# Sums of squares, gate projection and sample products of a two-layer hybrid decoder step: fewer, fuller matmuls, and a redrawn order

## The chip, the cores and the metric

The kernel runs on one core of a Trainium2 chip. The metric is the device time of one execution in microseconds (us); shorter is better. The core has a matrix engine (PE, with its weight loads listed apart as PEld), a vector engine (DVE), a scalar engine (ACT), a general engine (POOL) and a queue that issues the transfers (SP).

## What is computed

One inference step of a trunk with two layers, for 512 prompt tokens and 64 sample tokens (8 sequences of 8), 1024 channels wide, all in float32:

```
for i in 0, 1:
    h = rms_norm(x, norm_mix_pre[i])
    m = pool_mixer(h) if i == 0 else gdn_mixer(h)
    x = x + rms_norm(m, norm_mix_post[i])
    h = rms_norm(x, norm_ffn_pre[i])
    x = x + rms_norm(swiglu(h), norm_ffn_post[i])     # 2816 hidden channels
rms_norm(x, g) = x * rsqrt(mean(x * x) + 1e-6) * g
```

`gdn_mixer` projects h to q, k (8 heads of 128), v, z (16 heads of 128) and two gate columns per v head, runs a gated delta rule (for the prompt in chunks, with the inverse of a triangular matrix; for a sample group as one 64-row system on a given state) and projects back.

## The kernel before

Activations lie with channels on the 128 partitions and the 576 tokens along the free axis, cut into two halves (256 and 320 tokens, `HALVES`, or 288 and 288, `EVEN`). Every large product is three matmuls of rounded parts (`mm3`, line 882): a float32 operand is split into a high and a low part by ACT and DVE (`Weights.split`, line 874; `split2`, line 893), `hH`, `hL` for activations and `wh`, `wl` for weights. One such matmul is one record in the profile; a matmul on unsplit float32 operands is two records, shown as x2.

The program runs in stages: pooling mixer (0 to about 75 us), feed-forward 0 (to 445), GDN mixer with its four head groups G (to 1065), output projection and feed-forward 1 (to 1500), and the tail.

**Norms.** `add_sq` (line 901) squares eight channel blocks on ACT and adds the first seven into `nacc`; the eighth square stays in `nsq`. `rstd` (line 922) reduces both over the partitions with one-column matmuls against `ones`, two (256 tokens) or three (288, 320) places with two matmuls each, takes the root on ACT and the reciprocal on DVE (`nrc`), lays the result on a diagonal (`ndg`, two DVE operations) and spreads it to all partitions with one matmul `ones` x `ndg` into `ps_n`. It is called 12 times; `finish1` (line 2076) does the reduction alone, twice.

**Gates.** `gates` (line 1347) projects h on 32 columns (`wab`): 8 blocks of 3 matmuls into 32 partitions of `ps_g`, for each of the halves, then six small transposes of `abt`.

**Samples.** In `sample_front` (line 1585) the decay products take two matmuls on 64 rows (`gts` with the high and the low part of g), and k and q of the samples (`qks`) are multiplied by k and by `ident` in two column halves of the array each. In `sample_heads` (line 1649) `Ts` x `rs` are products on 64 rows. `Ts` is part of the tile `TQ`.

**The order.** The code only records operations. `Plan.finish` (line 389) then sets each engine's order with a list scheduler that has its own costs, starting from 40 random rounds and then refined once for each string in `CHOSEN` (four strings of window numbers and seeds, `refined`, line 438). Operations named `EITHER` go to DVE or POOL as it decides. Where the plan leaves PE waiting it puts matmuls `ps_w<-ones` that nobody reads (line 432). All recorded instructions are issued from line 436, so the profile is read by tile names.

Of the kernel before, what the change touches and what calls it, by code (L numbers as in the profile page):

```python
# [11 lines left out]
F32 = mybir.dt.float32  # L12
# [44 lines left out]
class Plan:  # L57
# [660 lines left out]
def hybrid_kernel(  # L718
# [69 lines left out]
    sp = pool("gsmp")  # L788

    bet = sp.tile([P, SP1, VH], F32, name="bet")  # L790
    gH = sp.tile([SMP, VH], F32R, name="gH")
    gL = sp.tile([SMP, VH], F32R, name="gL")
    ngs = sp.tile([P, SPANS, VH], F32, name="ngs")
    gce = sp.tile([P, SP1, VH], F32, name="gce")
# [23 lines left out]
    def masks(tmp):  # L818
# [22 lines left out]
        for h in range(2):  # L841
            q = slice(h * SMP, (h + 1) * SMP)
            DVE.tensor_tensor(s_st[q], s_in[q], ident[q, q], op=sub)
# [1285 lines left out]
```

## Time and profile before

| | |
|---|---|
| median of 3 runs | 1537.5 us (1536.16 to 1543.06) |
| profiled execution | 1546.52 us, span of its instructions 1544.5 us |
| PE, PEld busy | 98%, 95% of the span |
| DVE, ACT, POOL busy | 75%, 54%, 8% |
| instructions | 30415, of them 11879 PE records |

A row of the timeline gives the start, the length until the last of the merged instructions ends, engine, line, operation, the tile written, the tiles read, the shape and the count. Matmuls overlap: the time that one takes from its neighbours is read from its start to the start of the next one, not from its length. In the table by windows each engine has its busy time in the stretch and the number of its instructions; PEclk is the granted PE clock.

### The profile page before, as it was taken

To read this page: it belongs to the slowest core of one execution; us is meant where nothing else is said; L and a number is where in the kernel's file an instruction comes from. 1 tells how busy PE (TensorE), PEld (TensorE's weight loads), DVE (VectorE), ACT (ScalarE), POOL (GpSimd) and SP (SyncE) were. 2 spreads that over 40 slices of the span, in tenths; PEclk is the share of its full clock that TensorE was granted. 3 is DMA by queue.
4 is the path that set the end of the run, shared out by engine and by line. 5 is a ranking of instruction groups with operands and counts; after the bars stand their busy time and mean duration, and the time that the engine had idled before them with its cause. 6 is when DMAs were issued, how large, how long until landed. Compare 5 with 4: busy or idle time off the path is not lost.

```text
span 1544.5 us, 30415 instructions
## 1 busy us (share of the span) xinstructions
PE 1519.8 (98%) x11879; PEld 1465.1 (95%) x11879; DVE 1160.7 (75%) x2288; ACT 831.8 (54%) x1811; POOL 122.7 (8%) x265
## 2 busy tenths in 40 slices
PE   8999999999999999999999999999999999999998
PEld 7999999999999899899899889899999999999997
DVE  6794476658688698998899799557895576767854
ACT  7663443435455764854773764546564453534563
POOL 4210000000011010020121020100110000000000
PEclk9799999999999999999999999999999999999998
DMA  7364322333466533334433543657855433223262
GB/s 187 107 192 131 91 87 85 96 96 102 128 178 164 142 106 104 95 107 135 113 113 107 141 125 111 210 154 212 240 177 147 118 93 99 83 81 109 77 185 94
DMA packets 344902, 197.86 MB, mean 128 GB/s; under 512 B 13547, under 2 KB 337740, under 8 KB 344751
## 3 DMA queue, kind: packets, MB, share of 16 engines
q1 hardware_dynamic: 344759, 195.92, 44.4%
q8 instruction: 93, 1.52, 0.4%
q14 instruction: 50, 0.41, 0.1%
HBM read 165.60 MB, written 30.52 MB: 127 GB/s over the span
## 4 chain that ended last, share of the span: by engine, by line
PE 84%; DVE 10%; ACT 2%; DMA 2%; issue 1%; SPq 0%; DVEq 0%; ACTq 0%
PE ps_B L436 29%; PE ps_A L436 26%; PE ps_m L436 15%; PE ps_s L436 5%; PE ps_k L436 4%; PE ps_x L436 2%; PE ps_n L436 2%; DVE ia L436 2%; DVE wl L436 1%; PE ps_e L436 1%; DVE ii L436 1%; DVE ac L436 1%; DVE Uw L436 1%; PE ps_g L436 0%; DVE nacc L436 0%
## 5 line engine op out<-in xcount | busy, mean ns | idle before, releaser
L436 ACT ACTIVATE wh<-wraw 128x1024 fp32r<-128x1024 f32 (+4 forms) x240 | 233.0, 975 | 220.5 <-PE ps_B L436 82.5
L436 DVE TENSOR_TENSOR wl<-wraw,wh 128x1024 fp32r<-128x1024 f32 (+4 forms) x231 | 257.1, 1117 | 80.9 <-ACT wh L436 47.0
L436 PE MATMUL ps_m<-hH,wh 128*128 128x320 f32 (+1 forms) x832 | 246.4, 309 | 0.2 <-ACT u L436 0.2
L436 PE MATMUL ps_m<-hL,wh 128*128 128x320 f32 (+1 forms) x832 | 245.0, 306 | 0.0
L436 PE MATMUL ps_m<-hH,wl 128*128 128x320 f32 (+1 forms) x832 | 242.9, 307 | 0.3 <-DVE wl L436 0.3
L436 PEld LDWEIGHTS ps_m<-hH,wh 128*128 128x128 f32 x832 | 153.8, 188 | 4.3 <-issue 1.3
L436 PEld LDWEIGHTS ps_m<-hH,wl 128*128 128x128 f32 x832 | 152.8, 188 | 3.5 <-issue 1.4
L436 PEld LDWEIGHTS ps_m<-hL,wh 128*128 128x128 f32 x832 | 153.7, 188 | 2.3 <-issue 0.6
L436 PE MATMUL ps_B<-hL,wh 128*128 128x320 f32 (+1 forms) x444 | 128.2, 304 | 0.0
L436 PE MATMUL ps_B<-hH,wl 128*128 128x320 f32 (+1 forms) x444 | 128.0, 305 | 0.0
L436 PE MATMUL ps_B<-hH,wh 128*128 128x320 f32 (+1 forms) x444 | 127.7, 303 | 0.0
L436 PE MATMUL ps_A<-hH,wh 128*128 128x256 f32 (+1 forms) x432 | 119.3, 290 | 0.5 <-DVE nsq L436 0.5
L436 PE MATMUL ps_A<-hL,wh 128*128 128x256 f32 (+1 forms) x432 | 118.6, 290 | 0.0
L436 PE MATMUL ps_A<-hH,wl 128*128 128x256 f32 (+1 forms) x432 | 118.3, 289 | 0.0
L436 PE MATMUL ps_B<-aH,wl 128*128 128x288 f32 x352 | 99.3, 298 | 0.8 <-DVE wl L436 0.8
L436 PE MATMUL ps_B<-aL,wh 128*128 128x288 f32 x352 | 99.4, 296 | 0.0
L436 PE MATMUL ps_B<-aH,wh 128*128 128x288 f32 x352 | 98.5, 297 | 0.0
L436 PE MATMUL ps_A<-aH,wh 128*128 128x288 f32 x352 | 98.0, 296 | 0.0
L436 PE MATMUL ps_A<-aH,wl 128*128 128x288 f32 x352 | 97.9, 296 | 0.0
L436 PE MATMUL ps_A<-aL,wh 128*128 128x288 f32 x352 | 96.8, 295 | 0.0
L436 PEld LDWEIGHTS ps_B<-hH,wl 128*128 128x128 f32 x444 | 81.7, 188 | 0.9 <-DVE wl L436 0.4
L436 DVE SCALAR_TENSOR_TENSOR ac<-u,cwt,ac 128x600 f32<-128x600 f32 x96 | 80.4, 847 | 2.1 <-ACT ac L436 2.0
(462 smaller groups left out, 4076.2 us busy)
## 6 DMA issues: line engine op xcount, KB each, us to landing
wraw<-in_ffn_w_in_dram SPq DMA_DIRECT2D x77, 512.0 KB
wraw<-in_gdn_w_in_dram SPq DMA_DIRECT2D x56, 512.0 KB
graw<-in_ffn_w_in_dram SPq DMA_DIRECT2D x33, 512.0 KB
wraw<-in_ffn_w_out_dram SPq DMA_DIRECT2D x32, 448.0 KB
wraw<-in_gdn_w_out_dram SPq DMA_DIRECT2D x24, 512.0 KB
wraw<-in_ffn_w_out_dram SPq DMA_DIRECT2D x32, 320.0 KB
St<-in_state_gdn_rec_dram SPq DMA_DIRECT2D x32, 256.0 KB
out_dram<-St SPq DMA_DIRECT2D x32, 256.0 KB
```

Source lines behind the costliest of these rows:

```text
L436: calls[e](*a, **k)
```

## The change

1. `add_sq` adds the eighth square into `nacc` too; `rstd` and `finish1` have one matmul for each place. The diagonal `ndg` is gone: the column `nrc`, repeated 128 times, is the stationary operand of one matmul with `ident` for each block of up to 128 tokens.
2. `gates` loads `wab` by its own transfer and leaves it unsplit; four column groups of 32 take two channel blocks each, 16 float32 matmuls for a half. The turn and the sum over the four groups are six matmuls with `four`, four identities of 32 side by side.
3. Samples: high and low part of g lie on 128 rows (`gHL`), so one matmul does both; k of the samples is written twice side by side in `qks`, so each product is one matmul of the whole array; `rs` is written into `vs`, whose upper rows are zeroed at the start of each group, and is multiplied by the whole of `TQ`, whose corner is zeroed once.
4. `CHOSEN` has six strings with other numbers, so the whole order is redrawn.

```diff
@@ -77,112 +77,207 @@
     CHOSEN = (
-        "0: 67429 51633 92322 87354 32076 56101 80323 73026 43122 46420 11460 16617 76499; 1: 86614 42759 48104; "
...
+        "0: 51633 4180 93590 78750 34477 23530 63076 77272 88530 16072 91213 50029 90818 92607 6488 48788 652 "
@@ -829,8 +923,7 @@
         DVE.tensor_copy(s_gt2[:, SMP:], s_gt)
-        s_gt_r = cst.tile([SMP, P], F32R, name="s_gt_r")
-        DVE.tensor_copy(s_gt_r, s_gt2)
+        s_gt_r = cst.tile([P, P], F32R, name="s_gt_r")
@@ -841,6 +934,10 @@
             DVE.tensor_tensor(s_st[q], s_in[q], ident[q, q], op=sub)
+            for c in range(2):
+                DVE.tensor_tensor(s_gt_r[q, c * SMP:(c + 1) * SMP].rearrange("p (b t) -> p b t", b=NB),
+                                  t_gt[q, q].rearrange("p (b t) -> p b t", b=NB),
+                                  seqm2[q].unsqueeze(2).to_broadcast([SMP, NB, NT]), op=mult)
@@ -906,10 +1003,7 @@
             ACT.activation(sq, src, AF.Square)
-            if c == NC - 1:
-                acc.append(sq)
-            else:
-                EITHER.tensor_tensor(acc[0], acc[0], sq, op=add)
+            EITHER.tensor_tensor(acc[0], acc[0], sq, op=add)
@@ -921,28 +1015,25 @@
...
         for i, o in enumerate(offs):
-            for k, a in enumerate(acc):
-                PE.matmul(ps[:, i:i + 1], a[:, o:o + P], ones[:, 0:1], start=k == 0, stop=k == len(acc) - 1)
+            PE.matmul(ps[:, i:i + 1], acc[0][:, o:o + P], ones[:, 0:1], start=True, stop=True)
...
-        dg = halftile(tp, "ndg", hf, 1)
-        DVE.tensor_tensor(dg[:, :256].rearrange("p (i t) -> p i t", i=2), ident.unsqueeze(1).to_broadcast([P, 2, P]),
-                          rc[:, :2].unsqueeze(2).to_broadcast([P, 2, P]), op=mult)
-        if n > 256:
-            DVE.tensor_scalar(dg[:, 256:], ident[:, P - (n - 256):], rc[:, 2:3], None, op0=mult)
-        pr = bank("n%d" % hf.i)[:, :n]
-        PE.matmul(pr, ones, dg, start=True, stop=True)
+        pr = bank("n%d" % hf.i)[:, :hf.n]
+        for i in range(nb):
+            e = min((i + 1) * P, hf.n)
+            PE.matmul(pr[:, i * P:e], rc[:, i:i + 1].to_broadcast([P, P]), ident[:, i * P - offs[i]:e - offs[i]],
+                      start=True, stop=True)
@@ -1359,18 +1450,28 @@
             SP.dma_start(row[:, 1], gdn_dt_bias.to_broadcast([P, VH]))
-            wab = wts.load(w_in, 0, CONV + VDIM, NC, 2 * VH)
-            abt = cp_.tile([2 * VH, T], F32, name="abt", tag="ia", bufs=1)
+            wab = cp_.tile([P, NC, 2 * VH], F32, name="wab", tag="rs", bufs=2)
+            SP.dma_start(wab, w_in[:, CONV + VDIM:].rearrange("(k p) m -> p k m", p=P))
+            abt = cp_.tile([P, T], F32, name="abt", tag="ia", bufs=1)
+            four = cp_.tile([P, 2 * VH], F32, name="four", tag="sn", bufs=1)
+            i4 = ident.rearrange("p (q c) -> p q c", q=4)
+            DVE.tensor_tensor(four, i4[:, 0], i4[:, 1], op=add)
+            for q in (2, 3):
+                DVE.tensor_tensor(four, four, i4[:, q], op=add)
...
                 _, o0, n = hf
-                ps = bank("g")[:2 * VH, :n]
-                mm3(ps, wab, h_of(hf), NC)
+                ps = bank("g")[:, :n]
+                for i in range(4):
+                    for q in range(4):
+                        k = 2 * q + i // 2
+                        PE.matmul(ps[32 * q:32 * q + 32], wab[:, k], h_at(k, o0, n)[i % 2].bitcast(F32),
+                                  start=i == 0, stop=i == 3, tile_position=(0, 32 * q))
...
             for tt in range(SPANS):
-                PE.transpose(ps[:, tt], abt[:, tt * P:(tt + 1) * P], ident[:2 * VH, :2 * VH])
-            PE.transpose(ps[:SMP, SPANS], abt[:, SEQ:], ident[:2 * VH, :2 * VH])
-            PE.matmul(ps[SMP:, SPANS], abt[:, SEQ:], ident[:2 * VH, :2 * VH], start=True, stop=True)
+                PE.matmul(ps[:, tt], abt[:, tt * P:(tt + 1) * P], four, start=True, stop=True)
+            for q in range(2):
+                PE.matmul(ps[q * SMP:(q + 1) * SMP, SPANS], abt[:, SEQ:], four, start=True, stop=True)
@@ -1386,8 +1487,8 @@
                                      op0=mult, op1=mult)
-            DVE.tensor_copy(gH, g[:SMP, SPANS])
-            DVE.tensor_tensor(gL, g[:SMP, SPANS], gH.bitcast(F32), op=sub)
+            DVE.tensor_copy(gHL, g[:, SPANS])
+            DVE.tensor_tensor(gHL[SMP:], g[SMP:, SPANS], gHL[SMP:].bitcast(F32), op=sub)
@@ -1425,8 +1526,9 @@
             vt = gp.tile([P, SPANS, 4, P], F32, name="vt", tag="vt", bufs=2)
-            qks = gp.tile([P, 2, 2, SMP], F32, name="qks", tag="qks", bufs=2)
+            qks = gp.tile([P, 2, 3, SMP], F32, name="qks", tag="qks", bufs=2)
             vs = gp.tile([P, 4, P], F32, name="vs", tag="vs", bufs=2)
+            POOL.memset(vs[SMP:], 0.0)
@@ -1529,11 +1631,15 @@
                     qi = 0 if kind == "k" else 1
-                    dst, dss = qk[:, i, qi], qks[:, i, qi]
+                    dst, dss = qk[:, i, qi], qks[:, i, 2 * qi]
...
                 ACT.activation(dst, ac[:, :SEQ], AF.Silu)
-                ACT.activation(dss.rearrange("p (b t) -> p b t", b=NB), acs, AF.Silu)
+                if kind == "k":
+                    ACT.activation(qks[:, i, :2].rearrange("p x (b t) -> p x b t", b=NB),
+                                   acs.unsqueeze(1).to_broadcast([P, 2, NB, NT]), AF.Silu)
+                else:
+                    ACT.activation(dss.rearrange("p (b t) -> p b t", b=NB), acs, AF.Silu)
@@ -1581,17 +1687,17 @@
         E2 = [slice(0, SMP), slice(SMP, P)]
+        TQ = cp_.tile([P, 2, 2, P], F32, name="TQ")
+        POOL.memset(TQ[SMP:, :, :, SMP:], 0.0)
...
             ps = bank("s")[:, :4 * SMP].rearrange("p (h i) -> p h i", h=4)
-            gts = cp_.tile([SMP, 2, 4, SMP], F32R, name="gts", tag="T01", bufs=1)
-            for i, src in enumerate((gH, gL)):
-                gt = gts[:, i]
-                EITHER.tensor_tensor(gt, s_le.unsqueeze(1).to_broadcast([SMP, 4, SMP]),
-                                   src[:, h4].bitcast(F32).unsqueeze(2).to_broadcast([SMP, 4, SMP]), op=mult)
-                PE.matmul(ps, s_gt_r, gt, start=i == 0, stop=i == 1)
+            gts = cp_.tile([P, 4, SMP], F32R, name="gts", tag="T01", bufs=1)
+            EITHER.tensor_tensor(gts, s_in.unsqueeze(1).to_broadcast([P, 4, SMP]),
+                                 gHL[:, h4].bitcast(F32).unsqueeze(2).to_broadcast([P, 4, SMP]), op=mult)
+            PE.matmul(ps, s_gt_r, gts, start=True, stop=True)
@@ -1601,9 +1707,9 @@
                 pt = pk[:, P:2 * P]
-                for e, q in enumerate(E2):
-                    PE.matmul(pkv[q], qks[:, hd, 0], qks[:, hd], start=True, stop=True, tile_position=(0, e * SMP))
-                    PE.matmul(pt[q], qks[:, hd, 0], ident, start=True, stop=True, tile_position=(0, e * SMP))
+                kk = qks[:, hd, :2].rearrange("p x t -> p (x t)")
+                PE.matmul(pkv, kk, qks[:, hd, 1:], start=True, stop=True)
+                PE.matmul(pt, kk, ident, start=True, stop=True)
@@ -1674,7 +1780,8 @@
                 sn = cp_.tile([P, 4, 2, P], F32, name="sn", tag="sn", bufs=1)
-                rs, t1, vn = sn[lo, 0], sn[up, 1], sn[:, 2]
+                rss = vs[:, 2 * hd:2 * hd + 2]
+                rs, t1, vn = rss[lo], sn[up, 1], sn[:, 2]
@@ -1685,7 +1792,7 @@
                 for e in range(2):
-                    PE.matmul(pv[:, 0, e * P:(e + 1) * P], Ts[:, hd, e], rs[:, e], start=True, stop=True)
+                    PE.matmul(pv[:, 0, e * P:(e + 1) * P], TQ[:, hd, e], rss[:, e], start=True, stop=True)
@@ -2081,9 +2187,9 @@
                 n = n if i == 2 else P
-                for k, a in enumerate(acc):
-                    PE.matmul(ps[:n, i:i + 1], a[:, i * P:i * P + n] if i < 2 else a[:, EV - n:], ones[:, 0:1],
-                              start=k == 0, stop=k == len(acc) - 1)
+                a = acc[0]
+                PE.matmul(ps[:n, i:i + 1], a[:, i * P:i * P + n] if i < 2 else a[:, EV - n:], ones[:, 0:1],
+                          start=True, stop=True)
```

The array's work in the order, by kind: `ps_n<-ones,nsq` 38 matmuls before and none now; `ps_n<-ndg,ones` 12 and none; `ps_n<-ident,nrc` none and 32 (24 of 128 columns, 8 of 32 or 64); `ps_w<-ones` 31 and 42. ACT's table loads are 25 and 30.

PE at the first norm of the program (`ps_n_240`, `ps_n_244`: its reduction and its spread; `ps_B` belongs to the pooling of the second half), before:

```order
L436 MATMUL ps_n_240<-ones,nacc 128x1
L436 MATMUL ps_n_240<-ones,nsq 128x1
L436 MATMUL ps_B<-bm_146,xn 128x128
L436 MATMUL ps_B<-bh_148,xn 128x15
L436 MATMUL ps_B<-dH,wh 128x320
L436 MATMUL ps_B<-bm_146,xn 128x128 x2
L436 MATMUL ps_B<-bh_148,xn 128x15 x2
L436 MATMUL ps_B<-bm_146,xn 128x128
L436 MATMUL ps_B<-bh_148,xn 128x15
L436 MATMUL ps_B<-dL,wh 128x320
L436 MATMUL ps_B<-dH,wl 128x320
L436 MATMUL ps_n_244<-ndg,ones 128x256
```

The same norm now (`ps_n_239`, `ps_n_242`):

```order
L531 MATMUL ps_n_239<-ones,nacc 128x1
L531 MATMUL ps_B<-bm_145,xn 128x128
L531 MATMUL ps_n_239<-ones,nacc 128x1
L531 MATMUL ps_B<-dH,wh 128x320
L531 MATMUL ps_B<-bh_147,xn 128x15
L531 MATMUL ps_B<-bm_145,xn 128x128
L531 MATMUL ps_B<-dL,wh 128x320
L531 MATMUL ps_B<-dH,wl 128x320
L531 MATMUL ps_B<-bh_147,xn 128x15
L531 MATMUL ps_n_242<-ident,nrc 128x128 x2
```

The reductions over `nsq` are gone, and two matmuls with `nrc` stand in place of the one with `ndg`. PE in the gates, before (a stretch out of 24 such rows for the first half):

```order
L436 MATMUL ps_g<-hH,wl 32x256
L436 MATMUL ps_g<-hH,wh 32x256
L436 MATMUL ps_g<-hL,wh 32x256
L436 MATMUL ps_g<-hH,wl 32x256
L436 MATMUL ps_g<-hH,wh 32x256
```

and now, the whole of the first half:

```order
L531 MATMUL ps_m<-hH,wl 128x320
L531 MATMUL ps_g<-hH,wab 32x256 x4
L531 MATMUL ps_g<-hL,wab 32x256 x4
L531 MATMUL ps_g<-hH,wab 32x256 x4
L531 MATMUL ps_g<-hL,wab 32x256 x4
L531 MATMUL ps_x<-ident,qk 128x128 x4
```

Sixteen matmuls in runs of four stand for 24 single ones. PE at the samples' k and q of the first group, before:

```order
L436 MATMUL ps_m<-hL,wh 128x256
L436 MATMUL ps_k<-qks 64x128
L436 MATMUL ps_k<-ident,qks 64x128
L436 MATMUL ps_k<-qks 64x128
L436 MATMUL ps_k<-ident,qks 64x128
L436 MATMUL ps_k<-qks 64x128
L436 MATMUL ps_k<-ident,qks 64x128
L436 MATMUL ps_k<-qks 64x128
L436 MATMUL ps_k<-ident,qks 64x128
L436 MATMUL ps_m<-hH,wh 128x320
```

and now (the second pair of heads stands 53 rows further down):

```order
L531 MATMUL ps_k<-qk 128x256
L531 MATMUL ps_k<-qks 128x128
L531 MATMUL ps_k<-ident,qks 128x128
L531 MATMUL ps_m<-hH,wh 128x320
L531 MATMUL ps_m<-hL,wh 128x320
```

Two matmuls on all 128 columns take the place of four in column halves for each pair of heads.

More of the change, by code (lines that the diff above doesn't have):

```diff
@@ L790, in hybrid_kernel @@
     bet = sp.tile([P, SP1, VH], F32, name="bet")
-    gH = sp.tile([SMP, VH], F32R, name="gH")
-    gL = sp.tile([SMP, VH], F32R, name="gL")
+    gHL = sp.tile([P, VH], F32R, name="gHL")
     ngs = sp.tile([P, SPANS, VH], F32, name="ngs")
@@ L922, in rstd @@
     def rstd(tp, acc, hf, on_dve=False):
-        n = hf.n
-        offs = [0, P] if n == 256 else [0, P, n - P]
+        offs = [0, P] if hf.n == 256 else [0, P, hf.n - P]
+        nb = len(offs)
         ps = bank("n%d" % hf.i)
         for i, o in enumerate(offs):
-            for k, a in enumerate(acc):
-                PE.matmul(ps[:, i:i + 1], a[:, o:o + P], ones[:, 0:1], start=k == 0, stop=k == len(acc) - 1)
-        rc = halftile(tp, "nrc", hf, 1, (P, 4))[:, :len(offs)]
+            PE.matmul(ps[:, i:i + 1], acc[0][:, o:o + P], ones[:, 0:1], start=True, stop=True)
+        rc = halftile(tp, "nrc", hf, 1, (P, 4))[:, :nb]
         if on_dve:
-            v, t = (halftile(tp, w, hf, 1, (P, 4))[:, :len(offs)] for w in ("nv", "nt"))
-            DVE.tensor_scalar(v, ps[:, :len(offs)], 1.0 / D, EPS, op0=mult, op1=add)
+            v, t = (halftile(tp, w, hf, 1, (P, 4))[:, :nb] for w in ("nv", "nt"))
+            DVE.tensor_scalar(v, ps[:, :nb], 1.0 / D, EPS, op0=mult, op1=add)
             rsqrt(rc, v, t)
         else:
-            ACT.activation(rc, ps[:, :len(offs)], AF.Sqrt, bias=eps_c, scale=1.0 / D)
+            ACT.activation(rc, ps[:, :nb], AF.Sqrt, bias=eps_c, scale=1.0 / D)
             DVE.reciprocal(rc, rc)
-        dg = halftile(tp, "ndg", hf, 1)
-        DVE.tensor_tensor(dg[:, :256].rearrange("p (i t) -> p i t", i=2), ident.unsqueeze(1).to_broadcast([P, 2, P]),
-                          rc[:, :2].unsqueeze(2).to_broadcast([P, 2, P]), op=mult)
-        if n > 256:
-            DVE.tensor_scalar(dg[:, 256:], ident[:, P - (n - 256):], rc[:, 2:3], None, op0=mult)
-        pr = bank("n%d" % hf.i)[:, :n]
-        PE.matmul(pr, ones, dg, start=True, stop=True)
+        pr = bank("n%d" % hf.i)[:, :hf.n]
[3 more added lines that the diff above has]
+                      start=True, stop=True)
         return pr
@@ L1661, in sample_heads @@
                     EITHER.tensor_copy(kx.rearrange("p (b w) -> p b w", b=NB)[:, :, x_ * SMP:x_ * SMP + NT],
-                                    qks[:, hd, x_].rearrange("p (b t) -> p b t", b=NB))
+                                    qks[:, hd, 2 * x_].rearrange("p (b t) -> p b t", b=NB))
                 km = cp_.tile([P, NB, P], F32R, name="km", tag="T01", bufs=1)
@@ L1801, in core @@
             out.append(oss)
-            TQ = cp_.tile([P, 2, 2, P], F32, name="TQ", tag="TQ", bufs=1)
             Ts, Qs = TQ[:SMP], TQ[SMP:, :, :, :SMP]
```

305 rows, old and new, of the table CHOSEN are left out of this document.

## The prediction

> **What bounds the kernel now.** I read the page first: busy shares and the chain that ended last.
>
> ```profile
> span 1544.5 us, 30415 instructions
> PE 1519.8 (98%) x11879; PEld 1465.1 (95%) x11879; DVE 1160.7 (75%) x2288; ACT 831.8 (54%) x1811; POOL 122.7 (8%) x265
> ...
> PE 84%; DVE 10%; ACT 2%; DMA 2%; issue 1%; SPq 0%; DVEq 0%; ACTq 0%
> ```
>
> PE carries the end. So an edit counts by the PE time that it takes or gives, as long as nothing else ends last. Whether something does differs by stage. The table by windows, feed-forward 0, GDN mixer, feed-forward 1:
>
> ```profile
> 75.00:445.00 370.00, 369.40 (x2769) 367.55 (x2767) 254.03 (x399) 170.15 (x263) 5.27 (x6) 1.00 0.40 116
> 445.00:1065.00 620.00, 612.23 (x5163) 568.91 (x5163) 525.17 (x1209) 380.73 (x1055) 79.44 (x164) 1.00 0.47 133
> 1065.00:1500.00 435.00, 433.93 (x3274) 431.61 (x3274) 307.60 (x509) 212.35 (x340) 11.64 (x10) 1.00 0.45 132
> ```
>
> In the feed-forward stages the weight loader is busy 99% of the time (367.55 of 370.00, 431.61 of 435.00): PE time removed there is time saved. In the GDN stage PE is listed busy for 612 of 620 us, but the loader for 568.91, 92%; at the feed-forward's share it would be 616. Some 47 us of that stage are PE standing in pipelines, changing shape or waiting, and DVE has 525 us of work there. [...]
>
> A last reading concerns the clock, at the program's start:
>
> ```profile
> 18.00:45.00 27.00, 26.53 (x202) 24.22 (x201) 20.43 (x45) 22.49 (x61) 6.10 (x6) 1.00 0.48 111
> 45.00:62.50 17.50, 17.35 (x69) 15.93 (x69) 10.78 (x29) 9.05 (x25) 2.48 (x3) 0.51 0.32 96
> ```
>
> For 17.5 us the granted clock is half although PE is busy 99%. At full speed that work takes 17.5 x 0.51 = 8.9 us, so the stretch costs 8.6 us.
>
> The profiled execution took 1546.5 us, the median of the runs is 1537.5, 9.0 less. I make the sum against the profile and take it off the median unchanged, since a difference of kernels moves both.
>
> **The norms.** The last reduction of feed-forward 0's first half, three places with two matmuls each (rows between are left out), and its spread:
>
> ```profile
> 440.70 0.28 PE L436 MATMUL ps_n<-ones,nacc 128*128 128x1 f32 x2
> ...
> 441.73 0.36 PE L436 MATMUL ps_n<-ones,nsq 128*128 128x1 f32 x2
> 441.96 0.38 PE L436 MATMUL ps_B<-aL,wh 128*128 128x288 f32 x1
> ...
> 444.99 0.72 PE L436 MATMUL ps_n<-ndg,ones 128*128 128x288 f32 x2
> 445.34 0.51 PE L436 MATMUL ps_B<-aH,wl 128*128 128x288 f32 x1
> 445.69 0.42 PE L436 MATMUL ps_B<-aH,wh 128*128 128x288 f32 x2
> ```
>
> Six reductions take 441.96 - 440.70 = 1.26 us, 0.21 each. The groups show how many there are:
>
> ```profile
> L436 PE MATMUL ps_n<-ones,nsq 128*128 128x1 f32 (+2 forms) x76 | 13.6, 248 | 2.3 <-ACT nsq L436 2.3
> L436 DVE TENSOR_TENSOR ndg<-ident,nrc x12: 418/424/426, 35.6 to 1143.7; 128x256 f32<-128x256 f32 x12
> L436 DVE TENSOR_TENSOR nacc<-nacc,nsq x81: 406/453/2402, 20.7 to 1531.8; 128x288 f32<-128x288 f32 x36, 128x320 f32<-128x320 f32 x23, 128x256 f32<-128x256 f32 x22
> ```
>
> 76 records are 38 matmuls: 38 x 0.21 = 8.0 us removed. The spread before: 445.69 - 444.99 less one ordinary matmul of 0.13 is 0.57, for 12 norms 6.8. For the new spread, a float32 matmul of 128 columns, and below for four column groups, I use this place in the GDN stage:
>
> ```profile
> 620.62 1.93 PE L436 MATMUL ps_k<-St,kx 128*32 128x256 f32 x32
> 622.49 1.13 PE L436 MATMUL ps_k<-S,qk 128*128 128x256 f32 x4
> 623.45 0.61 PE L436 MATMUL ps_s<-vn,QD 128*128 128x128 f32 x4
> 623.90 0.49 PE L436 MATMUL ps_x<-ident,qk 128*128 128x128 f32 x3
> ```
>
> Two of 128 columns take 0.45, 0.225 each; two of 256 take 0.96, 0.48 each. The new spread is 24 x 0.225 + 8 x 0.21 = 7.1, so +0.3. No row loads a column repeated 128 times as weights: below, nothing is gained over an ordinary load, since the moving columns set these 0.225; above, I bound it by doubling, 32 x 0.21 = +6.7. [...] Norms: -7.7 on PE.
>
> On each norm's path one DVE addition of 0.453 comes ahead of the reduction and one `ndg` of 0.424 goes behind it, and half of the reductions go. That is even or a little shorter; beside it PE has other matmuls (441.96 onward), and without that cover it would be 14 x (0.45 - 0.42 - 0.5), a gain, so nothing is counted. DVE, which these queue on, gets 14 and loses 12 such operations.
>
> **The gates.** 48 matmuls in three groups of 16, one group, the step from one to the next, and the turn:
>
> ```profile
> L436 PE MATMUL ps_g<-hH,wl 128*32 128x256 f32 (+1 forms) x16 | 4.7, 294 | 0.0
> ...
> 490.22 0.28 PE L436 MATMUL ps_g<-hH,wh 128*32 128x256 f32 x1
> 490.34 0.28 PE L436 MATMUL ps_g<-hL,wh 128*32 128x256 f32 x1
> ...
> 510.28 0.69 PE L436 MATMUL ps_g<-ident,abt 32*128 32x32 f32 x7
> 510.90 0.42 PE L436 MATMUL ps_m<-hL,wh 128*128 128x320 f32 x1
> ```
>
> 24 of 256 columns at 0.12 and 24 of 320 at 0.14 (from 541.15 to 541.29, below) are 6.2 us. The new form is that of `St,kx`, 16 float32 matmuls of 256 columns in four column groups: 622.49 - 620.62 = 1.87 with the way out. For 320 columns 1.25 times that, 2.34, and twice 0.1 to get in (below): 4.4. The turn, 0.62 before, becomes six whole matmuls at 0.21, 1.3. Gates: 4.4 - 6.2 + 0.7 = -1.1. If the groups did not run side by side, 16 x 0.48 and 16 x 0.60 would be 17.3 us in place of 4.4. The split of `wab` on ACT and DVE goes, three additions for `four` come; neither is on PE's path. The SP queue has as many transfers as before.
>
> **The samples.** Three places of the first group: `gts`, with a run of idle matmuls behind it; `qks`; `TQ`.
>
> ```profile
> 541.15 0.31 PE L436 MATMUL ps_m<-hL,wh 128*128 128x320 f32 x1
> 541.29 0.30 PE L436 MATMUL ps_m<-hH,wl 128*128 128x320 f32 x1
> 541.53 0.50 PE L436 MATMUL ps_s<-gts,s_gt_r 64*128 64x256 f32 x2
> 541.96 0.43 PE L436 MATMUL ps_g<-misc,t_gt 128*128 128x64 f32 x2
> ...
> 542.64 0.94 PE L432 MATMUL ps_w<-ones 128*128 128x128 f32 x6
> 543.35 0.41 PE L436 MATMUL ps_m<-hH,wh 128*128 128x320 f32 x1
> ...
> 566.59 0.28 PE L436 MATMUL ps_m<-hL,wh 128*128 128x256 f32 x1
> 566.80 0.45 PE L436 MATMUL ps_k<-qks 128*64 128x128 f32 x4
> ...
> 567.87 0.41 PE L436 MATMUL ps_m<-hH,wh 128*128 128x320 f32 x1
> ...
> 624.14 0.36 PE L436 MATMUL ps_m<-hH,wh 128*128 128x256 f32 x1
> 624.44 0.71 PE L436 MATMUL ps_s<-sn,TQ 64*128 64x128 f32 x4
> 625.08 0.33 PE L436 MATMUL ps_x<-ident,qk 128*128 128x128 f32 x1
> ```
>
> From the last ordinary matmul to `gts` it is 0.24 where 0.14 is usual: 0.10 to change shape. `gts`: 0.10 + 0.43 becomes one matmul of 0.12, -0.4, four times -1.6. `qks`: 0.09 + 1.07 becomes four matmuls at 0.225, -0.27, four times -1.1. `TQ`: 0.30 - 0.12 + 0.64 becomes two at 0.225, -0.37, eight times -3.0. Samples: -5.7. POOL zeroes half of `vs` once a group, 512 columns as here:
>
> ```profile
> L436 POOL MEMSET eyo<- 128x512 f32 x1 | 0.5, 527 | 9.2 <-PE ps_n L436 9.2
> ```
>
> POOL has 79 us of work in the 620 of this stage and the rows are not needed until the products, so the memset is free; without that cover it is 4 x 0.53 = 2.1. Behind it on POOL queue the copies of the next projection.
>
> **The order.** 42 idle matmuls against 31: three take 543.35 - 542.64 = 0.71, so 11 more are 2.6 us in which the plan itself leaves PE waiting; 12 of them stand in the GDN stage, where the samples and gates are. I count +2.6. What else the redrawn order does no row of before shows: it may take back part of the 47 us, or add to them. I take zero between these. Five more table loads on ACT fall on an engine with 54% of work.
>
> **Sum.** -7.7 - 1.1 - 5.7 + 2.6 = -11.9: 1534.6 for an execution like the profiled one, and 1525.6 for the median.
>
> **The rivals.**
>
> A. The order takes stalls back in the GDN stage as well. For it: 47 us of loader slack there, in a stage in which the order decides what waits. Against: DVE has 85% of that stage in work. A fifth, 9.4 us, gives 1516; a third 1510.
>
> B. The GDN stage doesn't end by PE, and what gates and samples free becomes waiting for DVE. For it: the 12 more idle matmuls there. Only norms and idle matmuls stay: -5.1, 1532.4. This is within 0.5% of before (7.7 us, about what a measurement of this kernel can tell from no change).
>
> C. Slower: the new order leaves stretches so thin in PE work that the clock halves, as at 45 us, but in stages where PE is full. Each stretch like that one costs 8.6 us. Against the gain of 11.9 it decides from the second on; three are +25.8 - 11.9 = +13.9, 1551. For it: PE was busy 98% in the 27 us ahead of that stretch, so listed work doesn't protect. Against: from 75 to 1500 us the three windows show a clock of 1.00 throughout. [...]
>
> D. The change doesn't do what it says: the column groups run one behind the other. 17.3 - 4.4 = 12.9 more, 1538.5. Against: `St,kx` at 620.62.
>
> **How the numbers follow.** My forecast 0.47, A 0.27, B 0.17, C 0.06, D 0.03. The likeliest is the sum: 1525.6. Its own range, with the prices 30% off either way and part of the doubled weight load, is 1521 to 1531. The range adds A down to a loader gain of 15 us, 1511, and B with 3 us of order lost, 1536; C, D and the far end of A stay out, about 0.14. Faster than 1529.8: most of the forecast (0.44), all of A and a little of B, 0.72. Within 0.5%: the rest of the forecast, most of B, and D, 0.22. Slower: C, 0.06.
>
> **What would show it.** In the profile of the changed kernel: no `nsq` row on `ps_n`, `ident,nrc` x64 with about 0.225 from start to start for one matmul; `hH,wab` and `hL,wab` in two runs of about 1.9 and 2.3 us; single `gts`, pairs of `qks`; feed-forward 0 shorter by its norms' reductions only, about 1 us; the GDN stage shorter by some 7 us less the idle matmuls. A GDN stage shorter by over 12 us says A; one as long as before says B; a clock under 1.00 between 75 and 1500 us says C. The prediction is wrong if the feed-forward stages change by more than 5 us, or if the spread takes more than 0.3 a matmul.

## The result, and the profile after

| | before | after |
|---|---|---|
| median | 1537.73 us (4 runs, 1536.16 to 1543.06) | 1525.66 us (4 runs, 1525.06 to 1526.06) |
| profiled execution | 1546.52 us, span 1544.5 | 1525.06 us, span 1523.3 |
| granted clock of that execution | 0.986 | 0.997 |

The ratio is 0.9909 (0.988 to 0.9938 at 95%), so the kernel after is faster, and its median lies 0.06 us from the forecast of 1525.6. That the sum met the median so closely is partly luck, as the rest shows: the work gave about 3 us less than the sum, and the clock, which the sum counted at nothing, gave about 3 us.

The head of the page after, and its chain:

```profile
span 1523.3 us, 30379 instructions
PE 1501.0 (99%) x11850; PEld 1452.8 (95%) x11850; DVE 1155.7 (76%) x2284; ACT 840.6 (55%) x1815; POOL 129.4 (8%) x269
...
PE 88%; DVE 6%; ACT 3%; DMA 2%; issue 1%; POOL 0%; SPq 0%; DVEq 0%; ACTq 0%; POOLq 0%
```

PE still carries the end, 88% of the chain where it was 84%. The same three stretches of the table by windows:

```profile
75.00:445.00 370.00, 369.18 (x2759) 367.98 (x2759) 256.06 (x402) 172.90 (x266) 7.28 (x9) 1.00 0.39 113
445.00:1065.00 620.00, 613.95 (x5223) 574.59 (x5221) 520.86 (x1204) 387.24 (x1058) 84.10 (x162) 1.00 0.48 137
1065.00:1500.00 435.00, 432.94 (x3249) 430.00 (x3249) 306.61 (x502) 215.17 (x345) 11.98 (x13) 1.00 0.44 130
```

In the GDN stretch the loader has 574.59 us where it had 568.91, but the stretches are cut by time, and the one of after holds 16 us more of the output projection. Between the marks below the loader is busy for 544.61 of 594.28 us before and 546.00 of 591.10 after, so its slack there shrank by 4.6 us. The lengths of the stages are read from marks in the timeline: the first feed-forward product, the last `aH` product of feed-forward 0, the last `ps_m`, and the last group of matmuls. Before, then after:

```profile
60.53 0.41 PE L436 MATMUL ps_A<-hH,wh 128*128 128x256 f32 x1
...
467.45 0.30 PE L436 MATMUL ps_B<-aH,wl 128*128 128x288 f32 x1
...
1061.73 0.31 PE L436 MATMUL ps_m<-hH,wl 128*128 128x320 f32 x1
...
1536.64 1.38 PE L436 MATMUL ps_A<-ident,nh 128*128 128x128 f32 x6 [0.20 <-ACT nh L436]
```

```profile
50.74 0.39 PE L531 MATMUL ps_A<-hH,wh 128*128 128x256 f32 x1
...
454.65 0.30 PE L531 MATMUL ps_B<-aH,wl 128*128 128x288 f32 x1
...
1045.75 0.31 PE L531 MATMUL ps_m<-hH,wl 128*128 128x320 f32 x1
...
1515.46 0.95 PE L531 MATMUL ps_A<-ident,nh 128*64 128x128 f32 x6 [0.33 <-ACT nh L531]
```

How much of the difference is due to the clock can be read in the windows of before around its halved stretches, each shown with the 3.4 us ahead of it (the third column from the end is the granted clock):

```profile
41.90:45.30 3.40, 2.86 (x19) 2.21 (x17) 3.40 (x11) 2.97 (x9) 0.00 (x0) 1.00 0.00 0
45.30:62.40 17.10, 17.10 (x67) 15.74 (x68) 10.38 (x29) 8.65 (x23) 2.48 (x3) 0.50 0.32 97
468.60:472.00 3.40, 3.10 (x26) 2.88 (x26) 3.40 (x8) 2.38 (x6) 0.00 (x0) 1.00 0.46 133
472.00:475.40 3.40, 3.40 (x19) 3.40 (x18) 2.43 (x6) 0.38 (x1) 0.00 (x0) 0.50 0.78 202
1499.40:1502.80 3.40, 1.60 (x14) 1.38 (x12) 1.00 (x3) 1.37 (x3) 0.00 (x0) 1.00 0.88 230
1502.80:1509.60 6.80, 6.32 (x32) 6.16 (x33) 5.00 (x9) 2.96 (x7) 0.00 (x0) 0.50 0.31 90
```

After has nothing of the kind from 18 us to its last products:

```profile
18.00:1515.00 1497.00, 1487.27 (x11778) 1440.50 (x11776) 1140.46 (x2237) 827.94 (x1790) 115.86 (x196) 1.00 0.45 128
```

A stretch of 3.4 us would not show in the 1.00 of so long a window (the windows of the forecast hid the one at 472.0 in the same way); in windows of 10 us all those of after from 20 to 1510 us are at 1.00. Both kernels have one more at 11 us, 6.8 long, which cancels. A stretch at half clock costs half its length, if PE has work throughout: at 60.0 us of before a product of 320 columns starts 0.27 us ahead of the next, and 0.14 at full clock. So, in us:

| stage | before | after | difference | of it clock | rest |
|---|---|---|---|---|---|
| to the first feed-forward product | 60.5 | 50.7 | -9.8 | -7.6 | -2.2 |
| feed-forward 0 | 406.9 | 403.9 | -3.0 | -0.9 | -2.1 |
| GDN | 594.3 | 591.1 | -3.2 | -1.7 | -1.5 |
| output projection to the end | 474.9 | 469.7 | -5.2 | -3.4 | -1.8 |
| sum | | | -21.2 | -13.6 | -7.6 |

Of 21.2 us between the two profiled executions 13.6 are halved stretches that only before has. The median of before holds fewer of them. Its 75 runs beside the experiments, grouped by the granted clock that each run lists:

| granted clock | runs of before | median us |
|---|---|---|
| up to 0.9895 | 22 | 1544.9 |
| 0.990 to 0.9925 | 27 | 1539.4 |
| 0.993 to 0.9945 | 17 | 1535.4 |
| 0.995 and above | 9 | 1534.7 |

All ten runs of after (four above, six below) lie between 0.995 and 0.998, with a median of 1525.7. At about equal clock the change is worth 9.0 us, and 3 to 4 us more in the median come from the clock. The runs of after list up to 0.998 and those of before at most 0.996, so these 9.0 still hold a little clock; the traces leave 7.6.

The parts look as the change says. The groups of the norms' matmuls and one spread for 288 tokens, in the timeline:

```profile
L531 PE MATMUL ps_n<-ones,nacc 128*128 128x1 f32 (+2 forms) x76 | 9.7, 229 | 0.0
L531 PE MATMUL ps_n<-ident,nrc 128*128 128x128 f32 (+2 forms) x64 | 9.2, 271 | 0.0
```

```profile
433.79 0.86 PE L531 MATMUL ps_n<-ident,nrc 128*128 128x128 f32 x6
434.48 0.38 PE L531 MATMUL ps_B<-aH,wl 128*128 128x288 f32 x1
```

No row over `nsq` is left, and three spread matmuls take 0.69 us. The gates' two bursts, one `gts` and one pair `vs` x `TQ`:

```profile
502.99 0.64 PE L531 MATMUL ps_g<-hH,wab 128*32 128x256 f32 x8
...
504.86 0.55 PE L531 MATMUL ps_x<-ident,qk 128*128 128x128 f32 x3
...
508.46 0.75 PE L531 MATMUL ps_g<-hH,wab 128*32 128x320 f32 x8
...
510.76 0.44 PE L531 MATMUL ps_x<-ident,qk 128*128 128x128 f32 x2
...
527.48 0.34 PE L531 MATMUL ps_s<-gts,s_gt_r 128*128 128x256 f32 x1
...
612.14 0.75 PE L531 MATMUL ps_s<-vs,TQ 128*128 128x128 f32 x4
612.64 0.39 PE L531 MATMUL ps_m<-hH,wl 128*128 128x320 f32 x1
```

The bursts take 1.87 and 2.30 us (forecast 1.87 and 2.34); two products of `vs` with `TQ` take 0.50 (forecast 0.45).

### The profile page after: what moved, and what is told of

It reads as the page before. It is cut to its first block, busy times and chain, and to the rows that moved or that the text cites. A ratio compares the mean times of both kernels' runs of the same rounds, so it can differ in the third digit from the quotient of the medians.

```text
span 1523.3 us, 30379 instructions
## 1 busy us (share of the span) xinstructions
PE 1501.0 (99%) x11850; PEld 1452.8 (95%) x11850; DVE 1155.7 (76%) x2284; ACT 840.6 (55%) x1815; POOL 129.4 (8%) x269
## 4 chain that ended last, share of the span: by engine, by line
PE 88%; DVE 6%; ACT 3%; DMA 2%; issue 1%; POOL 0%; SPq 0%; DVEq 0%; ACTq 0%; POOLq 0%
PE ps_B L531 29%; PE ps_A L531 26%; PE ps_m L531 19%; PE ps_s L531 5%; PE ps_k L531 5%; PE ps_x L531 2%; PE ps_e L531 1%; DVE wl L531 1%; PE ps_n L531 1%; DVE Uw L531 1%; DMA vt<-z_d 1%; DVE ac L531 1%; ACT wh L531 1%; DMA wraw<-in_gdn_w_in_dram 0%; DMA yo<-y_d 0%
## 5 line engine op out<-in xcount | busy, mean ns | idle before, releaser
L531 PE MATMUL ps_m<-hH,wh 128*128 128x320 f32 (+1 forms) x832 | 251.5, 313 | 0.0
L531 PE MATMUL ps_m<-hH,wl 128*128 128x256 f32 (+1 forms) x832 | 245.8, 308 | 0.1
L531 PEld LDWEIGHTS ps_B<-hH,wh 128*128 128x128 f32 x444 | 81.7, 188 | 0.7 <-ACT wh L531 0.6
```

The lines of the kernel that those rows point to most:

```text
L531: calls[e](*a, **k)
```

## The experiments

**The theory after the result:** the edits free PE time at about the forecast prices; part of it is lost in waits; a second part of the gain is the clock, which from 18 us to the last products halves three times in before, each time behind 3.41 us in which PE moves few columns (1602 to 3084 by its rows, where the median is 7200), and not once in after. **Rivals:** the clock has nothing to do with it; the new order alone made the gain. Twelve kernels ran. Medians stand beside runs of before on the same chip: 1538.82 for e1 to e4, 1538.28 for e5 to e8, 1539.64 for e9 to e12.

### The kernel after once more

> The kernel after once more, unchanged, beside the variants on the same chip. Theory of the clock (half of the gain is PE work, the other half fewer stretches at half clock, which begin at different places from run to run): median 1525 to 1527 against 1538 to 1539 for before, granted clock 0.996 to 0.998 in nearly every run against 0.986 to 0.996 for before. Theory of PE work alone: the same medians, but the kernel before in its runs of the highest clock (0.995) is still 12 us above after. By the clock theory it is 6 to 9 us above after in such runs.

Measured: 1525.50 us (1524.24 to 1528.78), ratio to before 0.992 (0.989 to 0.9949); granted clock 0.995 or 0.996 in its six runs. Before's six runs beside it with 0.995 or more have a median of 1534.5. So the gain at about equal clock is 9, not 12: at the upper end of what the clock theory said. The clock has a part, and the work, edits and order together, has the larger one.

### Prices: one kind of matmul issued twice

Three kernels keep after's order and issue one kind of matmul twice.

```
 calls[e](*a, **k)
+if e == "PE" and self.twice(a):
+    calls[e](*a, **k)
...
+    return out == "ps_n" and l == "nacc"                                     # e1
+    return out == "ps_n" and l == "nrc"                                      # e2
+    return (out, l) in (("ps_k", "qks"), ("ps_s", "s_gt_r")) or (l, r) == ("TQ", "vs")   # e3
```

> The kernel after, in its own order, with each of the 38 one-column matmuls of the norms' reductions issued twice (the same value written twice): as many as the change removed, and at the places where the kept ones stand. Theory 1, PE is full and a matmul costs its own time: 38 x 0.21 = 8.0 us more than the kernel after (1525.7), 1533.7. Rival, the norms' matmuls stand where PE waits for a norm anyway, and the gain came from the order: under 2 us, 1526 to 1527.5. Rival, a norm's path carries them twice over (the matmul and the wait behind it): over 12 us, above 1537.

Measured: 1535.74 us (1531.55 to 1542.25), ratio to before 0.9988 (0.9968 to 1.0008). That is 10.2 over after, but its clock is lower too, 0.990 to 0.996. Its four runs at 0.995 and above have a median of 1534.2, which is 8.7 over after. The trace parts the two: its profiled execution is 15.0 us longer than that of after and holds four halved stretches of 3.4 us that after does not have (from 34.2, 51.3, 727.1 and 1498.5 us). They cost 6.8, and the rest is 8.2, close to the forecast price of 8.0. Two windows of it, and some rows of PE in the first:

```profile
30.80:34.20 3.40, 3.40 (x25) 2.96 (x24) 1.80 (x6) 1.56 (x6) 0.00 (x0) 1.00 0.33 91
34.20:37.60 3.40, 3.40 (x19) 3.40 (x17) 0.93 (x3) 1.32 (x4) 0.12 (x1) 0.50 0.02 5
```

```profile
32.78 0.29 PE L531 MATMUL ps_n<-ones,nacc 128*128 128x1 f32 x2
32.93 0.36 PE L533 MATMUL ps_n<-ones,nacc 128*128 128x1 f32 x2
33.16 0.47 PE L531 MATMUL ps_B<-bm,xn 128*128 128x128 f32 x2
33.46 0.28 PE L531 MATMUL ps_n<-ones,nacc 128*128 128x1 f32 x2
33.60 0.36 PE L533 MATMUL ps_n<-ones,nacc 128*128 128x1 f32 x2
```

PE is listed busy for 3.40 of 3.40 us and the clock halves all the same. What the window holds is work that moves little: reductions of one column each, and products of 64 columns ahead of them, 2278 columns in all by its rows, where the median of such windows in after is 7200. After, without the doubled rows, has a clock of 1.00 there. So the 38 one-column reductions cost 8.2 us of their own, 0.22 each, and beside them this trace lost 6.8 us to the clock.

> The kernel after, in its own order, with each of the 32 matmuls that spread a norm's root by a repeated column issued twice. Theory 1 with an ordinary weight load: 24 x 0.225 + 8 x 0.14 (a narrow one stands between starts 0.14 us apart in the trace of after), 6.5 us more, 1532.2. If a repeated column loads at double price: 13 us more or over, above 1538. If the spread hides in a wait for the norm: under 2 us, below 1527.7.

Measured: 1533.48 us (1530.99 to 1538.04), ratio 0.9972 (0.9955 to 0.9989), median clock 0.996: 8.0 over after, 0.25 for each of the 32 and 1.5 more than the forecast. In the trace one halved stretch more (from 725.7 us) costs 1.7 of the 8.3 us by which its profiled execution is longer; the 6.6 left are 0.21 for each and the forecast of 6.5. So a repeated column loads at about the ordinary price; double price is out.

> The kernel after, in its own order, with the samples' products on whole rows issued twice: 4 of gts, 16 of qks and 16 of vs with TQ, where a product that adds to a bank adds twice (so the samples' part of the output counts double). Theory 1, the GDN stage ends by PE: 4 x 0.12 + 32 x 0.225 = 7.7 us more, 1533.4, all of it between the first gate matmul and the last of ps_m. Rival B, the stage waits for DVE and what PE is given hides: under 2.5 us, 1526 to 1528.

Measured: 1532.52 us (1531.18 to 1535.12), ratio 0.9958 (0.9941 to 0.9974), median clock 0.996: 7.0 over after, forecast 7.7. None of these products adds to what its bank holds, so nothing counts twice in the output. The marks of its GDN stage:

```profile
454.82 0.29 PE L531 MATMUL ps_B<-aH,wl 128*128 128x288 f32 x1
...
1053.63 0.31 PE L531 MATMUL ps_m<-hH,wl 128*128 128x320 f32 x1
```

598.8 us where after has 591.1: 7.7 more, the whole of the forecast, with no halved stretch in the stage of either. What is added to PE in this stage counts in full.

### The idle matmuls, taken away and added

```
 if e is None:
-    self.tc.nc.tensor.matmul(self.banks[i[0]][i[1]][0][:, :self.idle.shape[1]], self.idle, self.idle,
-                             start=True, stop=True)
     continue
```

> The kernel after, in its own order, without its 42 idle matmuls, which write a bank that nothing reads. Theory 1, they stand where the plan leaves PE waiting: between no change (1525.7) and 42 x 0.235 = 9.9 us less (1515.8); by the prediction's count, a quarter of their time on the path, some 2.5 us less, 1523. Rival, they hold the clock: without them the granted clock falls below 1.00 in the GDN stage, 8.6 us for a stretch like the one at 45 us of the kernel before, so 1534 or more.

Measured: 1534.33 us (1531.58 to 1541.15), ratio 0.9966 (0.9947 to 0.9986): 8.8 slower than after with 42 matmuls less, and no run with a clock over 0.994. Two of the four halved stretches in its trace before the end, with the windows ahead of them:

```profile
462.90:466.30 3.40, 2.52 (x21) 2.20 (x19) 3.40 (x7) 1.54 (x4) 0.00 (x0) 1.00 0.29 80
466.30:469.70 3.40, 3.40 (x17) 3.40 (x17) 3.40 (x7) 1.08 (x3) 2.61 (x3) 0.50 0.94 254
531.20:534.60 3.40, 1.94 (x11) 1.32 (x10) 3.40 (x10) 3.36 (x6) 0.92 (x2) 1.00 0.66 191
534.60:538.00 3.40, 3.40 (x17) 3.40 (x17) 2.84 (x14) 2.77 (x7) 1.20 (x3) 0.50 0.85 233
```

The four last 20.4 us together and cost 10.2. The start is no different from that of after, although the page lists no halved stretch there: time ahead of the first record of the clock counts as full. The rows show half speed until 15.8 us, 0.21 us from start to start and then 0.12:

```profile
14.96 0.41 PE L529 MATMUL ps_A<-dL,wh 128*128 128x256 f32 x1
15.17 0.41 PE L529 MATMUL ps_A<-dH,wl 128*128 128x256 f32 x1
...
18.76 0.28 PE L529 MATMUL ps_A<-dL,wh 128*128 128x256 f32 x1
18.88 0.28 PE L529 MATMUL ps_A<-dH,wl 128*128 128x256 f32 x1
```

So the clock accounts for the whole of the 9.6 us between the two profiled executions, and the 42 matmuls themselves cost 10.2 less 9.6, some 0.6 us. The idle matmuls hold the clock, as the rival has it: 0.984 to 0.994 in the twelve runs without them, 0.995 to 0.998 in those of after. What they cost, the 0.6 us, is small beside the 10.2.

The other way round: before, with idle matmuls added where its trace shows thin stretches.

```
 if e in (None, "PE"):
+    for _ in range(self.MORE.get(at, 0) if e else 0):
+        self.more(still, quiet)
+    at += 1
...
+MORE = {186: 2, 188: 1, 400: 2, 3385: 2, 3393: 1, 5921: 6, 10590: 8}
```

> The kernel before in its own order, with 22 more idle matmuls at five places where its trace shows PE waiting and moving few columns (43.3, 82.6, 469.2, 855.2 and 1503.3 us). Nothing else changes. Theory of the clock: thin stretches, in which PE moves few columns within about 3.4 us, halve the clock for the next stretch, and filled ones don't: the granted clock rises to 0.995 or more and the median falls by 4 to 8 us from before's, to 1531 to 1534. Theory of PE work: 22 more matmuls cost between nothing (they stand in waits) and 22 x 0.22 = 4.8 us, the clock stays at 0.992 or so: 1538 to 1543.

Measured: 1536.31 us (1534.24 to 1538.39), ratio 0.9981 (0.9962 to 1.0001). The clock is 0.993 to 0.997 in its twelve runs, and the spread shrinks from 15.3 us in before to 4.2. Three of the five places lie where before's trace was halved; the same three here:

```profile
40.00:62.40 22.40, 22.25 (x170) 20.83 (x169) 21.23 (x60) 16.73 (x41) 3.81 (x5) 1.00 0.48 141
466.00:475.40 9.40, 9.40 (x80) 9.14 (x79) 8.46 (x20) 5.64 (x9) 3.46 (x6) 1.00 0.59 158
1495.00:1510.00 15.00, 15.00 (x122) 14.95 (x121) 9.43 (x16) 6.10 (x11) 0.00 (x0) 1.00 0.56 182
```

All at full clock. So the filled stretches kept the clock in this trace, as the clock theory has it, while the size of the effect was taken too large: the median fell by 2.0, which its interval does not tell from nothing, and not by 4 to 8, since before's median loses some 4 us to the clock, against its runs at 0.995 and above, and the added matmuls cost 1 to 2.

### PE work taken from before, in its own order

```
+if out == "ps_n" and l == "nsq":                                          # e7
+    continue
...
+    thin += 1                                                             # e8, at ps_m<-hH,wl
+    if thin % 16 == 8 and not k["stop"] and not k["start"]:
+        continue
```

> The kernel before in its own order, without the 38 one-column matmuls on the eighth squares (the norms then lack one eighth of their sum). PE work: 38 x 0.21 = 8.0 us less than before, some 1530.5. If these matmuls, which keep PE listed busy and move one column each, also made stretches thin: 2 to 4 us more than that, 1527 to 1529, with the granted clock up to 0.994 or more. If the norms wait for the last square anyway: under 3 us, 1536 or more.

Measured: 1536.88 us (1528.73 to 1541.43), ratio 0.9983 (0.9959 to 1.0006): 1.4 less in the median, and 8.0 less (0.9948) lies outside the interval. Its five runs at 0.995 and above have a median of 1531.0, 3.5 below before's beside them at such clocks, but they spread from 1528.7 to 1538.0. So about half of the 8.0 came through, as far as five runs tell. The clock did not get better: its trace still halves at 45.2 and 468.4 us.

> The kernel before in its own order, without 38 of the 832 correction products of the GDN stage's projection, spread evenly over the stage (21 of 320 columns, 17 of 256). If that stage ends by PE, it gets shorter by 21 x 0.14 + 17 x 0.12 = 5.0 us and the whole falls to 1533.5; what the change gave less than its sum in this stage was then lost by the new order. Rival B, the stage waits for DVE: under 1.5 us less, 1537 or more, and the change could not have had its sum there in any order.

Measured: 1533.38 us (1531.07 to 1540.37), ratio 0.9972 (0.9948 to 0.9995): 4.9 less, as expected if that stage ends by PE. But its four runs at 0.995 and above are at 1532.2, 2.3 below before's, and in its trace the GDN stage is no shorter. Its marks, and the longest entry of PE's waits in that stage, here and in before:

```profile
466.12 0.30 PE L443 MATMUL ps_B<-aH,wl 128*128 128x288 f32 x1
...
1060.04 0.31 PE L443 MATMUL ps_m<-hH,wl 128*128 128x320 f32 x1
```

```profile
PE ps_x L443 <- DVE vt L443: 3.5, 5, 1.2
```

```profile
PE ps_x L436 <- DVE vt L436: 1.6, 1, 1.6
```

593.9 us against 594.3, of which 1.7 were clock. PE waits 3.5 us for `vt` where it waited 1.6. One trace and four runs don't settle the share, between none and all of the 5.0; at equal clock it is about half, and what can be seen of the rest is waits, for DVE above all. Rival B has its part in that.

### Without the refinement

Four kernels with `CHOSEN = ()`: before, after, and before with one edit alone.

> The kernel before with CHOSEN empty: its operations in the order of the 40 random rounds alone, without the refinement by windows. It is the base of the next three. Slower than before by what the refinement gave, which no run shows yet: 1540 to 1600.

Measured: 1563.07 us (1560.66 to 1565.68), ratio to before 1.0153 (1.012 to 1.0186). The refinement of before's order gave 23.4 us.

> The kernel after with CHOSEN empty: the edits of the change in an order that nobody refined. Theory 1, the edits free PE and an order drawn for them turns that into time: 7 to 12 us below the unrefined kernel before. Theory 2, the refinement of the new order made the gain, and the edits alone give nothing: within 3 us of the unrefined kernel before, or slower; two unrefined orders may differ by some us on their own, so between 3 and 7 us stays undecided.

Measured: 1583.26 us (1578.84 to 1585.66), ratio to before 1.0283 (1.0253 to 1.0314): 20.2 slower than the unrefined kernel before. The refinement of after's order gave 58 us. Theory 1 fails in this form: the edits alone, in the order that 40 random rounds happen to find, lose.

> The unrefined kernel before with the norms' edit alone (one reduction a place, the repeated column). In before's fixed order the removal of the reductions gave some 3 us at equal clock, and PE waited for the rest. Theory 1, a newly drawn order uses the rest too: 6 to 8 us below the unrefined kernel before. Rival, the norm's path ends the wait in any order: under 3 us.

Measured: 1565.30 us (1563.26 to 1567.79), ratio to before 1.0168 (1.0136 to 1.02): 2.2 slower than its base, whose runs go from 1560.66 to 1565.68. The ranges overlap, so no difference is shown, and the gain of 6 to 8 us of theory 1 is not there.

> The unrefined kernel before with the samples' edit alone (gts on 128 rows, qks written twice, rs in the zeroed vs times the whole TQ). By the price of the products 5.7 us less; by what the GDN stage kept of a removal in before's order, 0 to 3 us less; theory 2, order alone: anywhere within 5 us of the unrefined kernel before, either way.

Measured: 1581.07 us (1579.93 to 1582.40), ratio to before 1.027 (1.0238 to 1.0302): 18.0 slower than its base, outside of what any theory said. About 5 of the 18 are clock, since its trace holds halved stretches of 17.1 us in all behind the start and that of its base 6.8. No price of a product explains the rest. The four times fall in two pairs: 1563.07 and 1565.30 without the samples' edit, 1583.26 and 1581.07 with it. The idle matmuls go the same way, 75 and 75 against 121 and 108, and say that the plan itself left PE waiting more. Whether the random rounds drew worse orders by chance, or the samples' edit brings dependences that any unrefined order pays for, no run parts; other seeds were not tried, nor the gates' edit alone. The GDN stage of the two whole kernels, e9 and then e10, cut close to its marks:

```profile
465.00:1075.00 610.00, 594.07 (x5006) 547.83 (x5007) 502.01 (x1163) 365.69 (x1021) 72.34 (x145) 1.00 0.45 126
```

```profile
465.00:1090.00 625.00, 605.29 (x5049) 557.06 (x5048) 502.99 (x1150) 371.80 (x1024) 76.73 (x163) 0.99 0.44 122
```

By its marks the stage is 14 us longer in the unrefined after (626.99 against 613.03), about 5 of them clock, and the loader is busy for 90% and 89% of it, where the refined kernels have 92%. Unrefined orders differ by more than all edits together, so these four can't price an edit. They show that the order can be a term as large as any other, and that the forecast's zero for it had no run behind it. What stays open: whether before with six strings of its own would have come down as well. No run tried it, so the 9.0 us at equal clock can't be parted into edits and order.

## Why the prediction was right, and where it was wrong

- **What bounds the kernel:** held for work that is added. PE time put into the full order counts at its price (beside the clock, the profiled executions give 8.2 of 8.0 in e1, 6.6 of 6.5 in e2 and 7.8 of 7.7 in e3). It held by about half for work that is taken out of a fixed order (e7, e8): PE then meets the next wait. The 47 us of slack in the GDN stage were the author's estimate from the loader's share; the 7.7 us of e3, put into that stage, came out whole all the same.
- **The norms, -7.7:** prices right. No row of before showed how a repeated column loads, so the ordinary load in the sum was the author's choice. Reductions take 0.21; the spread takes 0.23 in the timeline and 0.21 to 0.25 in e2, about an ordinary load. The three stages with norms and without gates or samples lost 2.2, 2.1 and 1.8 us beside the clock, 6.1 together, of which the idle matmuls and the order are not parted.
- **The gates, -1.1, and the samples, -5.7:** bursts and products as priced, but the GDN stage became only 1.5 us shorter beside the clock, where 6.8 less 2.6 for idle matmuls was forecast. This is where the sum is short.
- **Idle matmuls, +2.6:** the term took them for waits that the new plan adds. Outside of its records PE has 24.7 us before (1544.5 less 1519.8) and 22.3 after (1523.3 less 1501.0). With the idle matmuls' own time, below, that is 36.8 and 36.7: no wait was added. And what they do for the clock is worth far more than they cost (10.2 us against some 0.6, e4).

```profile
L432 PE MATMUL ps_w<-ones 128*128 128x128 f32 x62 | 12.1, 343 | 1.3 <-POOL ones L211 1.3
L527 PE MATMUL ps_w<-ones 128*128 128x128 f32 x84 | 14.4, 300 | 1.3 <-POOL ones L306 1.3
```

- **The order, zero:** not supported. Refinement is worth 58 us in after and 23 in before; how much of the measured gain the redrawn order carries stays open.
- **"I make the sum against the profile and take it off the median unchanged, since a difference of kernels moves both":** this is the step that failed. The profiled execution of before held 13.6 us of halved clock that after doesn't have. The stretch at 45 us was seen and priced at 8.6, and then counted as common to both kernels. The clock of 1.00 "throughout" from 75 to 1500 us was a misreading: windows of 370 to 620 us round away the 3.4 us at 472.0. Sum and median met because the work gave 9.0 or a little less in place of 11.9 and the clock gave 3 to 4 in place of 0.
- **Rival A** (GDN shorter by over 12): no, 3.2. **B** (GDN as long as before): in part right; the stage gave 1.5 us beside the clock, and in before's order e8 lost about half of its 5.0. **D** (serial column groups): no, 1.87 and 2.30 us.
- **Rival C** (thin stretches halve the clock): so it was in before, at 45.3, 472.0 and 1502.8 us, and not in after. Listed work ahead did not keep the clock: the window at 41.9 us of before is busy 2.86 of 3.40, the one at 30.8 us of e1 has no gap at all, and both have a halved one behind them, so the clock deserved a term of its own, with both signs.
- **What would have made it wrong:** the stage with feed-forward 1, from the output projection to the end, changed by 5.2 us, over the 5 that was named for a feed-forward stage; 3.4 of it is the stretch at 1502.8.

## What to carry to other kernels

Before a profiled execution is compared with anything, list its stretches below full clock and price them: here they were 13.6 of 21.2 us, and runs of before that differ by 15 us differ in their listed clock too (1532.84 us at 0.996, 1548.12 at 0.985). Use short windows, since long ones round a stretch away (3.4 us at half clock leave 1.00 in a window of 620). Doubling an operation gives its price in the present order, and taking it away tells what the order lets through; where a planner sets the order, only a redrawn and refined order tells what an edit is worth. Work that keeps an engine listed busy while little moves through it can be dearer than its time: in e1 the doubled reductions took 8.2 us, and the trace was 15.0 longer.

## What the runs showed of the hardware

- In the traces of before and after, the halved stretches that end ahead of the last products last 3.41, 6.83 and 17.07 us. How much of an execution they take differs from run to run of the same code: the 75 runs of before list a clock of 0.985 to 0.996.
- From 18 us to the last products, before has three windows of 3.41 us at full clock with a halved one behind (from 41.9, 468.6 and 1499.4 us). By the rows of PE they move 2398, 3084 and 1602 columns, where the median of such windows moves 7200, in before as in after. The columns alone do not tell: two more windows of before, with 2936 and 2680 (from 24.8 and 35.1 us), and six of after, with 2182 to 3008, have full clock behind them. What decides stays open. PE's busy time tells less: it is 2.86, 3.10 and 1.60 us of 3.40 in the three of before, and 3.40 in the one at 30.8 us of e1.
- With 22 idle matmuls at five places, e6, the clock of before went from 0.992 to 0.996 in the median.
- A weight load of one column repeated 128 times showed about the ordinary price: 0.21 to 0.25 us for each spread matmul, where a float32 matmul of 128 columns in before had 0.225.
